# Log-sum-exp of 16,384 rows: another layout of the rows over the partitions, and two stores for one

## Chip, cores and metric

One core of a Trainium2 chip. The metric is device time in microseconds of one execution. Timed runs of one kernel mostly lie within 0.3 us of their median, so that small differences are told by the ratio over several rounds with its 95% interval.

## The reference

```python
# x: (32, 512, 1024) float32, standard normal; result (32, 512)
max_x = np.max(x, axis=-1, keepdims=True)
return (max_x.squeeze(-1) + np.log(np.sum(np.exp(x - max_x), axis=-1))).astype(np.float32)
```

16,384 rows of 4 KiB are read once, 67.1 MB; 64 KB are written.

## The kernel before

The kernel sums plain exponentials, with no maximum taken off, and checks at the end that no sum left the safe range; only if one did would a branch do the exact computation. Each of the 128 partitions owns 128 consecutive rows, 512 KiB of memory; this distance from the first row of one partition to that of the next is called the pitch here. Seventeen groups of rows (16, 16, 16, 15, 14, 10, 9, 8, 6, 4, 4, 3, 2, 2, 1, 1, 1 rows per partition) pass through a ring of 48 rows: SyncE issues the load, ScalarE takes exponentials in place, VectorE or ScalarE's own accumulator forms the sums.

```python
x_rows = x_flat.rearrange("(p c) d -> p c d", p=P)
out_view = out.rearrange("a b -> (a b)").rearrange("(p c) -> p c", p=P)
...
EARLY = 104
...
def load(p0, c0, size):
    step = 4 if c0 in (32, 48) else 1        # third and fourth load in four parts
    return [
        nc.sync.dma_start(
            out=ring[k::step, p0 : p0 + size, :], in_=x_rows[k::step, c0 : c0 + size, :]
        ).ins
        for k in range(step)
    ]
...                                          # in the loop over the loads:
    if c == EARLY + 14:
        nc.scalar.activation(out=res[:, 0:EARLY], in_=sumexp[:, 0:EARLY], func=AF.Ln)
...                                          # after the loop:
nc.scalar.activation(out=res[:, EARLY:NC], in_=sumexp[:, EARLY:NC], func=AF.Ln)
nc.sync.dma_start(out=out_view, in_=res)
```

Two logarithms fill the result: one over columns 0 to 103, taken while the last loads are still coming, one over the last 24 at the very end.

Of the kernel before, what the change touches and what calls it, by code (L numbers as in the profile page):

```python
# [14 lines left out]
def kernel(  # L15
# [5 lines left out]
    nc = tc.nc  # L21
    P = nc.NUM_PARTITIONS
# [6 lines left out]
    x_flat = x.flatten_outer_dims()  # L29
    n, d = x_flat.shape  # L30
    assert n % P == 0
    NC = n // P
    H = d // 2

    x_rows = x_flat.rearrange("(p c) d -> p c d", p=P)
    out_view = out.rearrange("a b -> (a b)").rearrange("(p c) -> p c", p=P)



# [2 lines left out]
    loads = [  # L42
        "R8 R8", "R8 R8", "R8 R8", "R7 R6 A A", "R6 R5 A A A", "R5 R4 A", "R5 R4", "R5 T3",
        "R3 A A A", "R3 A", "R2 T2", "R3", "R1 A", "T2", "T1", "A", "A",
    ]
    loads = [[(op[0], int(op[1:] or 1)) for op in load.split()] for load in loads]
    assert sum(s for ops in loads for _, s in ops) == NC
    ENGINES = [mybir.EngineType.Activation, mybir.EngineType.DVE]
    EARLY = 104
    LATE = 118  # L50
    LAST = NC - 1
# [5 lines left out]
    ring = big.tile([P, RING, d], fp32, name="ring")  # L57
    sumexp = stats.tile([P, NC], fp32, name="sumexp")
    res = stats.tile([P, NC], fp32, name="res")
# [9 lines left out]
    nc.vector.memset(ones, 1.0)  # L69
    nc.vector.memset(far, 100 * HIGH)  # L70

    def load(p0, c0, size):


        step = 4 if c0 in (32, 48) else 1
        return [
            nc.sync.dma_start(
                out=ring[k::step, p0 : p0 + size, :], in_=x_rows[k::step, c0 : c0 + size, :]
            ).ins
            for k in range(step)  # L80
        ]

    def without_wait(ins, group, reason):

        tc.declare_no_dep(ins.ins, group=group, reason=reason)


    def check(c0, c1, i):
        nc.vector.tensor_scalar(  # L89
            out=clamped[:, c0:c1], in0=sumexp[:, c0:c1],  # L90
            scalar1=LOW, scalar2=HIGH, op0=ALU.max, op1=ALU.min,
        )
        nc.vector.scalar_tensor_tensor(  # L93
            out=clamped[:, c0:c1], in0=clamped[:, c0:c1], scalar=0.0, in1=sumexp[:, c0:c1],
            op0=ALU.bypass, op1=ALU.not_equal, accum_out=bad[:, i : i + 1],
        )
        nc.tensor.matmul(count, lhsT=bad[:, i : i + 1], rhs=far, start=i == 0, stop=False)  # L97

    c = 0
    p = 0  # L100
    for ops in loads:
        size = sum(s for _, s in ops)
        if p + size > RING:
            p = 0
        dmas = load(p, c, size)
        if c == 0:
            first_load = dmas[0]
        for how, s in ops:
            v = ring[:, p : p + s, :]
            sums = sumexp[:, c : c + s]  # L110
            if how == "A":
                o = v if c < LAST else last_exp
                exp = nc.scalar.activation(out=o, in_=v, func=AF.Exp, accum_out=sums)  # L113
            else:
                exp = nc.scalar.activation(out=v, in_=v, func=AF.Exp)  # L115
            without_wait(exp, "loads", "the slot's earlier users came before this load")
            without_wait(exp, "exps", "the slot's earlier users came before this load")
            without_wait(exp, "sums", "the slot's earlier users came before this load")
            tc.add_to_no_dep_group("exps", exp.ins)
            added = []  # L120
            if how == "R":
                added = [nc.vector.reduce_sum(out=sums, in_=v, axis=AX.X)]  # L122
            elif how == "T":
                for r in range(s):
                    lo = ring[:, p + r, 0:H]
                    added.append(
                        nc.vector.scalar_tensor_tensor(  # L127
                            out=lo, in0=lo, scalar=1.0, in1=ring[:, p + r, H:d],
                            op0=ALU.mult, op1=ALU.add, accum_out=sums[:, r : r + 1],
                        )  # L130
                    )
            for add in added:
                for dma in dmas:
                    tc.declare_no_dep(add.ins, dma, reason="ScalarE has waited for it")
                without_wait(add, "loads", "they came before this one")
            for add in added:
                tc.add_to_no_dep_group("sums", add.ins)
            c += s
            p += s
            last_row = v  # L140
        for dma in dmas:
            tc.add_to_no_dep_group("loads", dma)
        if c == EARLY + 14:
            nc.scalar.activation(out=res[:, 0:EARLY], in_=sumexp[:, 0:EARLY], func=AF.Ln)  # L144
        if c == LATE + 3:
            check(0, LATE, 0)

    def start_early(program):
# [13 lines left out]
    nc.at_finalize(start_early)  # L162

    nc.scalar.activation(out=res[:, EARLY:NC], in_=sumexp[:, EARLY:NC], func=AF.Ln)  # L164
    nc.sync.dma_start(out=out_view, in_=res)



# [3 lines left out]
        out=bad[:, 2:3], in0=bad[:, 3:4], scalar1=LOG_LOW, scalar2=None, op0=ALU.is_lt  # L172
# [4 lines left out]
    all_fine = nc.values_load(  # L177
        fine[0:1, 0:1], engines=ENGINES, min_val=0, max_val=1,
        skip_runtime_bounds_check_because="a truth value",
    )  # L180
    with tc.If(all_fine < 1, preferred_fallthrough_block=False):
        with tc.tile_critical(sync_engine=mybir.EngineType.Activation):
            with nc.semaphore("landed") as landed, nc.semaphore("ready") as ready:
                rows = 0
                steps = 0
                for c0 in range(0, NC, RING):
                    s = min(RING, NC - c0)
                    v = ring[:, 0:s, :]
                    neg = clamped[:, c0 : c0 + s]
                    if c0:  # L190
                        nc.scalar.wait_ge(ready, steps)
                    nc.scalar.dma_start(out=v, in_=x_rows[:, c0 : c0 + s, :]).then_inc(landed, 16)
                    rows += 16
                    nc.vector.wait_ge(landed, rows)
                    nc.vector.tensor_reduce(
                        out=neg, in_=v, op=ALU.max, axis=AX.X, negate=True
                    ).then_inc(ready, 1)
                    nc.vector.wait_ge(ready, steps + 1)
                    nc.vector.tensor_add(
                        out=v, in0=v, in1=neg[:, :, None].to_broadcast([P, s, d])  # L200
                    ).then_inc(ready, 1)
                    nc.scalar.wait_ge(ready, steps + 2)
                    nc.scalar.activation(out=v, in_=v, func=AF.Exp).then_inc(ready, 1)
                    nc.vector.wait_ge(ready, steps + 3)
                    nc.vector.reduce_sum(
                        out=sumexp[:, c0 : c0 + s], in_=v, axis=AX.X
                    ).then_inc(ready, 1)
                    steps += 4
                nc.scalar.wait_ge(ready, steps)
                nc.scalar.activation(out=res, in_=sumexp, func=AF.Ln).then_inc(ready, 1)  # L210
                nc.vector.wait_ge(ready, steps + 1)
                nc.vector.tensor_sub(out=res, in0=res, in1=clamped).then_inc(ready, 1)
                nc.scalar.wait_ge(ready, steps + 2)
                nc.scalar.dma_start(out=out_view, in_=res).then_inc(landed, 16)
                nc.scalar.wait_ge(landed, rows + 16)


# [28 lines left out]
```

## Time and profile before

| | before |
|---|---|
| time, median (3 runs at first; 6 with the later ones) | 164.42 us (164.14 us) |
| span of the profiled run | 162.2 us |
| busy: DMA queue / VectorE / ScalarE | 96.8% / 75% / 72% |
| loads, first packet to last | 1.01 to 157.92 us |
| store issued, SyncE goes on after it | 159.80, 161.35 us |

The DMA queue is what is full; the two compute engines follow it.

### The profile page before, as it was taken

What the parts mean: (1) busy time and instruction counts of PE and PEld (TensorE: products, weight loads), DVE (VectorE), ACT (ScalarE), POOL (GpSimd) and SP (SyncE); (2) the same over time, 40 slices, a digit from 0 to 9 for tenths busy, and PEclk for the clock granted to TensorE, in tenths of its full rate; (3) what the DMA queues carried; (4) which work ended last, traced back from release to release, by engine and by line L of the source; (5) the groups of instructions that cost most, each with busy time, mean ns of one, the idle gap of its engine ahead of it and who ended that gap; (6) DMA issues with size and microseconds to landing.
All of it is one profiled execution on the core that took longest, in us unless ns stands there. A gap on an engine that the chain in (4) does not pass through costs nothing.

```text
span 162.2 us, 216 instructions
## 1 busy us (share of the span) xinstructions
PE 0.6 (0%) x8; PEld 0.3 (0%) x8; DVE 122.3 (75%) x47; ACT 116.8 (72%) x53; POOL 0.2 (0%) x4
## 2 busy tenths in 40 slices
PE   0000000000000000000000000000000000000001
PEld 0000000000000000000000000000000000000000
DVE  0000000799959999499999995999998999979993
ACT  3000049990799709994499839999969599999993
POOL 0000000000000000000000000000000000000000
DMA  7997997997997999999999999999999999999980
GB/s 259 517 453 323 517 501 307 485 517 323 453 517 323 453 501 394 394 424 485 453 453 396 410 422 414 414 432 436 436 420 436 426 424 410 436 421 411 413 338 20
DMA packets 2690, 67.19 MB, mean 414 GB/s; under 512 B 384, under 2 KB 512, under 8 KB 896
## 3 DMA queue, kind: packets, MB, share of 16 engines
q1 hardware_dynamic: 2688, 67.18, 96.8%
q14 instruction: 2, 0.02, 0.0%
HBM read 67.11 MB, written 0.07 MB: 414 GB/s over the span
## 4 chain that ended last, share of the span: by engine, by line
DMA 64%; DVE 22%; ACT 12%; issue 0%; PE 0%; DVEq 0%
DMA ring<-in_x_dram 64%; DVE sumexp L122 21%; ACT ring L115 12%; DVE ring L127 1%; PE count L174 0%; DVE clamped L89 0%; DVE bad L171 0%; DVE bad L170 0%; DVE clamped L93 0%; DVE fine L176 0%; PE count L175 0%; DVEq L89 0%
## 5 line engine op out<-in xcount | busy, mean ns | idle before, releaser
L122 DVE TENSOR_REDUCE sumexp<-ring 128x8 f32<-128x8192 f32 (+7 forms) x20 | 116.1, 5854 | 36.2 <-ACT ring L115 36.2
L115 ACT ACTIVATE ring<-ring 128x8192 f32<-128x8192 f32 (+7 forms) x24 | 101.7, 4283 | 42.2 <-DMA ring<-in_x_dram 42.2
L113 ACT ACTIVATE ring<-ring 128x1024 f32<-128x1024 f32 x12 | 12.5, 1040 | 0.0
L127 DVE SCALAR_TENSOR_TENSOR ring<-ring 128x512 f32<-128x512 f32 x8 | 5.1, 686 | 0.0
L113 ACT ACTIVATION_READ_ACCUMULATOR ring<-ring 128x1 f32 x12 | 2.2, 186 | 0.0
L68 ACT ACT_TABLE_LOAD x1 | 1.3, 1283 | 0.8 <-PEq L230 0.8
L113 ACT ACTIVATE last_exp<-ring 128x1024 f32<-128x1024 f32 x1 | 1.0, 1013 | 0.0
L97 PE MATMUL count<-far,bad 128*1 128x1 f32 x4 | 0.4, 164 | 159.1 <-DVE clamped L93 159.1
L69 DVE MEMSET ones<- 128x1 f32 x1 | 0.1, 59 | 0.9 <-PEq L230 0.9
L127 DVE DVE_READ_ACCUMULATOR ring<-ring 128x1 f32 x8 | 0.7, 84 | 0.0
L93 DVE SCALAR_TENSOR_TENSOR clamped<-clamped,sumexp 128x118 f32<-128x118 f32 (+1 forms) x2 | 0.5, 226 | 0.1
L89 DVE TENSOR_SCALAR clamped<-sumexp 128x118 f32<-128x118 f32 (+1 forms) x2 | 0.4, 198 | 0.1
L97 PEld LDWEIGHTS count<-far,bad 128*1 128x1 f32 x4 | 0.2, 81 | 159.2 <-DVE clamped L93 159.2
L176 DVE TENSOR_SCALAR fine<-count 1x1 int32<-1x1 f32 x1 | 0.1, 147 | 0.3 <-PE count L175 0.3
L144 ACT ACTIVATE res<-sumexp 128x104 f32<-128x104 f32 x1 | 0.3, 272 | 0.0
L164 ACT ACTIVATE res<-sumexp 128x24 f32<-128x24 f32 x1 | 0.2, 223 | 0.0
L170 DVE TENSOR_REDUCE bad<-ring 128x1 f32<-128x64 f32 x1 | 0.2, 220 | 0.0
L174 PE MATMUL count<-far,bad 128*1 128x1 f32 x2 | 0.2, 164 | 0.2 <-DVE bad L171 0.2
L175 PE MATMUL count<-ones,sumexp 128*1 128x1 f32 x2 | 0.2, 164 | 0.0
L113 ACT ACTIVATION_READ_ACCUMULATOR last_exp<-ring 128x1 f32 x1 | 0.2, 186 | 0.0
L171 DVE TENSOR_SCALAR bad<-bad 128x1 f32<-128x1 f32 x1 | 0.2, 154 | 0.0
L93 DVE DVE_READ_ACCUMULATOR clamped<-clamped,sumexp 128x1 f32 x2 | 0.2, 82 | 0.0
(7 smaller groups left out, 0.7 us busy)
## 6 DMA issues: line engine op xcount, KB each, us to landing
ring<-in_x_dram SPq DMA_DIRECT2D x4, 1920.0 KB, 24.8
ring<-in_x_dram SPq DMA_DIRECT2D x1, 7168.0 KB, 30.1
ring<-in_x_dram SPq DMA_DIRECT2D x1, 5120.0 KB, 31.3
ring<-in_x_dram SPq DMA_DIRECT2D x1, 4608.0 KB, 33.7
ring<-in_x_dram SPq DMA_DIRECT2D x1, 4096.0 KB, 29.3
ring<-in_x_dram SPq DMA_DIRECT2D x2, 2048.0 KB, 32.7
ring<-in_x_dram SPq DMA_DIRECT2D x1, 3072.0 KB, 36.2
ring<-in_x_dram SPq DMA_DIRECT2D x2, 1024.0 KB, 38.8
```

What stands on the lines that cost most here:

```text
L68: nc.scalar.preload_act_table_set("natural_log_exp_and_others")
L89: nc.vector.tensor_scalar(out=clamped[:, c0:c1], in0=sumexp[:, c0:c1], scalar1=LOW, scalar2=HIGH, op0=ALU.max, op1=ALU.min,)
L93: nc.vector.scalar_tensor_tensor(out=clamped[:, c0:c1], in0=clamped[:, c0:c1], scalar=0.0, in1=sumexp[:, c0:c1], op0=ALU.bypass, op1=ALU.n ...
L97: nc.tensor.matmul(count, lhsT=bad[:, i : i + 1], rhs=far, start=i == 0, stop=False)
L113: exp = nc.scalar.activation(out=o, in_=v, func=AF.Exp, accum_out=sums)
L115: exp = nc.scalar.activation(out=v, in_=v, func=AF.Exp)
L122: added = [nc.vector.reduce_sum(out=sums, in_=v, axis=AX.X)]
L127: nc.vector.scalar_tensor_tensor(out=lo, in0=lo, scalar=1.0, in1=ring[:, p + r, H:d], op0=ALU.mult, op1=ALU.add, accum_out=sums[:, r : r + 1],
L144: nc.scalar.activation(out=res[:, 0:EARLY], in_=sumexp[:, 0:EARLY], func=AF.Ln)
L164: nc.scalar.activation(out=res[:, EARLY:NC], in_=sumexp[:, EARLY:NC], func=AF.Ln)
L170: nc.vector.reduce_max(out=bad[:, 3:4], in_=last_row[:, 0, 0 : d // 16], axis=AX.X)
L171: nc.vector.tensor_scalar(out=bad[:, 2:3], in0=bad[:, 3:4], scalar1=LOG_LOW, scalar2=None, op0=ALU.is_lt)
```

## The change

Each partition now owns 120 consecutive rows, a pitch of 480 KiB, from the first 15,360 rows; the last 1,024 rows are given out 8 per partition and are read as the eighth load, into columns 0 to 7. The result then lies in two regions of the output, hence two stores, of 32 and 480 bytes per partition. The intent is to get the 128 streams off a pitch that is a large power of two. The splits of the third to fifth load change from 4, 4, 1 parts to 4, 2, 2.

```diff
-    x_rows = x_flat.rearrange("(p c) d -> p c d", p=P)
-    out_view = out.rearrange("a b -> (a b)").rearrange("(p c) -> p c", p=P)
+    B = 8
+    W = NC - B
+    x_rows = x_flat[0 : P * W].rearrange("(p c) d -> p c d", p=P)
+    x_rest = x_flat[P * W : n].rearrange("(p c) d -> p c d", p=P)
+    out_flat = out.rearrange("a b -> (a b)")
+    out_rows = out_flat[0 : P * W].rearrange("(p c) -> p c", p=P)
+    out_rest = out_flat[P * W : n].rearrange("(p c) -> p c", p=P)
...
-        step = 4 if c0 in (32, 48) else 1
+        step = {2: 4, 3: 2, 4: 2}.get(i, 1)
...
+        if i == REST:                     # REST = 7
+            c = 0
+        else:
+            c = following                 # starts at B
+            following += size
...
-    nc.sync.dma_start(out=out_view, in_=res)
+    nc.sync.dma_start(out=out_rest, in_=res[:, 0:B])
+    nc.sync.dma_start(out=out_rows, in_=res[:, B:NC])
```

The early logarithm's condition now counts `following`, and with it still comes after the same load.

More of the change, by code (lines that the diff above doesn't have):

```diff
@@ L48 @@
     ENGINES = [mybir.EngineType.Activation, mybir.EngineType.DVE]
+    REST = 7
     EARLY = 104
@@ L70, with source, load @@
     nc.vector.memset(far, 100 * HIGH)
-    def load(p0, c0, size):
-        step = 4 if c0 in (32, 48) else 1
+    def source(c0, size):
+        assert c0 >= B or (c0 == 0 and size == B)
+        return x_rows[:, c0 - B : c0 - B + size, :] if c0 >= B else x_rest
+    def load(p0, c0, size, i):
+        step = {2: 4, 3: 2, 4: 2}.get(i, 1)
         return [
             nc.sync.dma_start(
-                out=ring[k::step, p0 : p0 + size, :], in_=x_rows[k::step, c0 : c0 + size, :]
+                out=ring[k::step, p0 : p0 + size, :], in_=source(c0, size)[k::step]
             ).ins
@@ L97, in check @@
         nc.tensor.matmul(count, lhsT=bad[:, i : i + 1], rhs=far, start=i == 0, stop=False)
-    c = 0
+    following = B
     p = 0
-    for ops in loads:
+    for i, ops in enumerate(loads):
         size = sum(s for _, s in ops)
@@ L104 @@
             p = 0
-        dmas = load(p, c, size)
-        if c == 0:
+        if i == REST:
[3 more added lines that the diff above has]
+            following += size
+        dmas = load(p, c, size, i)
+        if i == 0:
             first_load = dmas[0]
@@ L142 @@
             tc.add_to_no_dep_group("loads", dma)
-        if c == EARLY + 14:
+        if following == EARLY + 14:
             nc.scalar.activation(out=res[:, 0:EARLY], in_=sumexp[:, 0:EARLY], func=AF.Ln)
-        if c == LATE + 3:
+        if following == LATE + 3:
             check(0, LATE, 0)
@@ L191 @@
                         nc.scalar.wait_ge(ready, steps)
-                    nc.scalar.dma_start(out=v, in_=x_rows[:, c0 : c0 + s, :]).then_inc(landed, 16)
-                    rows += 16
+                    for c1, s1 in ((0, B), (B, s - B)) if c0 == 0 else ((c0, s),):
+                        nc.scalar.dma_start(
+                            out=ring[:, c1 - c0 : c1 - c0 + s1, :], in_=source(c1, s1)
+                        ).then_inc(landed, 16)
+                        rows += 16
                     nc.vector.wait_ge(landed, rows)
@@ L213 @@
                 nc.scalar.wait_ge(ready, steps + 2)
-                nc.scalar.dma_start(out=out_view, in_=res).then_inc(landed, 16)
-                nc.scalar.wait_ge(landed, rows + 16)
+                nc.scalar.dma_start(out=out_rest, in_=res[:, 0:B]).then_inc(landed, 16)
+                nc.scalar.dma_start(out=out_rows, in_=res[:, B:NC]).then_inc(landed, 16)
+                nc.scalar.wait_ge(landed, rows + 32)
 _INS = ['x']
```

## The prediction

> **What bounds the kernel now.** I began with the page's strip of 40 slices and the totals of the DMA queue, because the change is about the addresses that the loads read.
>
> ```profile
> DMA  7997997997997999999999999999999999999980
> DMA packets 2690, 67.19 MB, mean 414 GB/s; under 512 B 384, under 2 KB 512, under 8 KB 896
> q1 hardware_dynamic: 2688, 67.18, 96.8%
> HBM read 67.11 MB, written 0.07 MB: 414 GB/s over the span
> ```
>
> The reader is to see 96.8%: the 16 DMA engines have packets in flight for all but 5.2 us of the 162.2 us. (The 7s in the first third alternate with 9s because whole 64 KB packets are booked at one point; the same effect gives impossible shares over 1 in short windows.) So I asked for longer stretches, cut where the packet sizes change:
>
> ```profile
> core 0: us, PE busy (x) PEld busy (x) DVE busy (x) ACT busy (x) POOL busy (x), PEclk, DMA share, GB/s
> 0.00:4.50 4.50, 0.00 (x0) 0.00 (x0) 0.09 (x2) 1.28 (x1) 0.20 (x4) 1.00 0.92 320
> 4.50:46.00 41.50, 0.00 (x0) 0.00 (x0) 16.62 (x2) 18.32 (x3) 0.00 (x0) 1.00 1.01 439
> ...
> 46.00:61.00 15.00, 0.00 (x0) 0.00 (x0) 12.97 (x3) 9.57 (x2) 0.00 (x0) 1.00 1.00 433
> ...
> 95.50:140.00 44.50, 0.00 (x0) 0.00 (x0) 42.02 (x13) 40.67 (x20) 0.00 (x0) 1.00 0.99 428
> 140.00:151.00 11.00, 0.00 (x0) 0.00 (x0) 10.04 (x10) 10.97 (x11) 0.00 (x0) 1.00 0.99 419
> ```
>
> Only two stretches are below some 430 GB/s: the first 4.5 us, and the end, where packets shrink to 16, 8 and 4 KB. The single packet records of the trace say why. A 64 KB packet takes 2.418 us in the steady part, which is 27.1 B/ns on one engine, 433.7 GB/s on 16; the 384 packets of that size are all within 0.05 us of it except the first one on each engine (16 of them, 2.97 to 3.46 us, mean 3.22) and one second packet (2.57). A 16 KB packet takes 0.615 us (26.7 B/ns), a 4 KB one 0.161 (25.4), so each packet has some 10 ns of its own. If every packet took the steady time of its size, an engine would be busy 155.54 us; it is busy 156.50 on average. Loads start at 1.01 and end at 157.92, 156.91 us apart. So all that the load stream loses against its own steady speed is about 1 us, 0.81 of it in the first packet (3.22 less 2.42).
>
> Next, is the queue ever empty, or does a compute engine hold it up? The waits of the issuing queue:
>
> ```profile
> SPq L77 <- DVE sumexp L122: 86.0, 7, 24.3
> SPq L77 <- DMA ring<-in_x_dram: 38.6, 4, 18.4
> SPq L165 <- ACT res L164: 18.7, 1, 18.7
> ```
>
> The issuer waits 86.0 us for the reduction that frees ring rows, and yet the engines don't run dry: the fourth load is issued at 46.68 us while the third is landing until about 60.6, and the fifth at 66.00 while the fourth lands until 78.8. The slack is 13 to 14 us, so an issue that is a microsecond earlier or later changes nothing. The chain of waits agrees: 64% of it is DMA, and its DVE and ACT pieces are only the route by which a ring slot was freed.
>
> The last thing is what follows the loads. In order of time:
>
> ```profile
> 158.38 1.01 ACT L113 ACTIVATE last_exp<-ring 128x1024 f32<-128x1024 f32 x1
> ...
> 159.55 0.22 ACT L164 ACTIVATE res<-sumexp 128x24 f32<-128x24 f32 x1
> ...
> 159.80 0.35 SPq L165 DMA_DIRECT2D out_dram<-res  x1
> ```
>
> and the queue's waits after 159 us:
>
> ```profile
> SPq L241 <- ACTq L181: 0.3, 1, 0.3
> SPq L241 <- DMA out_dram<-res: 0.2, 1, 0.2
> ```
>
> The store is issued at 159.80; its packets (27 ns each) run from 160.64 to 161.00, and SyncE, after the branch of the other engines, still waits 0.2 us for it and goes on at 161.35. From there 0.85 us of closing barrier lead to 162.2. So the store's landing is on the path that sets the end, with a slack of only -0.2 us.
>
> **What the Trainium skill says.** "DMA: Bandwidth & Descriptors", section "Latency and other measured facts", has the reason for the change: at a per-partition row pitch of 512 KiB, copies from HBM to HBM ran at 207 GB/s per direction, against 214 at a pitch padded by 4 KiB (with 103 at 4 MiB). This kernel's pitch is 128 rows x 4 KiB = 512 KiB; the change makes it 120 x 4 KiB = 480 KiB. Taken as it stands that is 3% of the load stream. The trace doesn't agree that it is lost here: at 512 KiB the loads run at 433.7 GB/s. The same page, section "Where 436 GB/s comes from", puts the ceiling of the ports into SBUF at 435.2 GB/s; the trace's steady 433.7 is 99.7% of that, so no memory layout has more than 0.3% to give in the steady part. (In the copies there is no SBUF port in the way and both sides have the pitch.) The page's "Specifications" give about 0.6 us to the first byte on this path, which is most of the 0.81 us by which the first packets are longer, and say that transfers under 512 B need a read-modify-write; the store before is of exactly 512 B per partition, and no run so far shows a smaller one to HBM.
>
> **The change part by part.**
> 1. Pitch 480 instead of 512 KiB for 15 of the 16 load groups, and 8 rows per partition (32 KiB each, contiguous) from the tail of the input as the eighth load. Row sizes, order of sizes and ring slots are the same: the load of 8 rows was the eighth before too. So the packets have the same sizes and the steady part takes the same. Possible gain: only the 0.81 us of the start, where all 16 engines begin together on addresses with equal low bits. By the 0.6 us of the skill, about 0.2 of it could be conflict; by the trace alone, anything from 0 to 0.81. I choose 0.25. It would pass through in full, because every later landing, slot and issue moves with it.
> 2. Splits. The third load stays in four parts; the fourth goes from four parts to two, the fifth from one to two: 22 load issues for 23. A further issue costs SyncE 0.33 to 0.6 us, with 13 us of slack. The semaphore that each issue reuses moves by one, to older loads mostly. Worth 0.
> 3. Compute: the same tiles on the same engines; sums, logs and checks are taken at the same places in the sequence (the eighth load now fills columns 0 to 7, still inside the first 104). Worth 0.
> 4. Two stores for one. The 32-byte one goes first, at 159.80 less the gain; the 480-byte one follows it on the same queue. Issues back to back in this trace start 0.37 to 0.48 us apart (113.399, 113.770, 114.249 us), and the second of such a pair takes 0.10 us longer than one alone (0.434 against 0.328). The second store's landing is therefore later by about 0.40, perhaps 0.50. The 128 packets of 32 B take eight places per engine, at 10 to 27 ns each at most 0.2 us, but they run while the second issue is still being written, so none of it adds. A read-modify-write, if it shows, adds perhaps 0.1. As the old landing was already what SyncE waited for, all of it counts: +0.45.
> 5. The branch with the exact maximum is not taken and its instructions cost nothing here beyond what they cost before.
>
> Sum: -0.25 + 0 + 0 + 0.45 = +0.20 us on 164.42, which is 164.62. I say 164.6.
>
> **Rivals.**
> - *The pitch does cost bandwidth, as in the copies.* 3% of 156.9 us would be -4.7 us, some 160.2 with the store. For it: the skill's measurement at this very pitch, and that somebody thought it worth a change. Against it: packets of one size that vary by 0.05 us in 156 us, at the rate of the SBUF ports. A conflict would show as spread. I give it 3%.
> - *The first packets are slow through conflict altogether.* Then 0.8 us come back and the time is 164.42 - 0.8 + 0.45 = 164.1. The first 16 packets' spread (2.97 to 3.46) speaks for it a little; that a first packet must bear the latency which later ones hide behind their predecessors speaks against.
> - *The stores cost more.* If the small writes make the landing wait, the old 1.2 us from issue to the last completion packet may become 2: 164.42 + 1.0 to 1.3 = 165.4 to 165.7. No packet under 512 B other than completion writes is in the trace, so I can't exclude it.
> - *Two parts instead of four load the SBUF ports unevenly.* Another grouping of partitions per engine could slow packets of the fourth and fifth loads, 29 of 128 rows. Against it: the third and fourth loads in four parts ran at 433 GB/s, as fast as the unsplit ones. If it came, 10% of 35 us would be 3.5 us, but slack doesn't help a busy DMA: 168. I give it 2%.
>
> **Range and chances.** The likely terms are a gain of 0 to 0.8 and a cost of 0.35 to 1.0, so -0.45 to +1.0; the three runs before spread over 0.30 us. That gives 163.9 to 165.3 for 8 times in 10. Two per cent is 3.29 us: faster needs a time under 161.13, which only the first rival gives; slower needs 167.71, which only the last one gives. Hence 0.03, 0.95, 0.02.
>
> **What would show it.** In the changed profile the loads' 64 KB packets still take 2.42 us and the rate from 4.5 to 140 us stays at 428 to 439 GB/s (step 1); if it rises above 436 over a long stretch, the ceiling is not what I take it for. The stretch 0 to 4.5 us, now 320 GB/s, shows the gain at the start: 64 KB packets of 2.97 to 3.46 us become shorter or don't. The fourth and fifth loads keep their packet durations (step 2). The last exponential begins near 158.1 (step 3). Two issues of the store 0.35 to 0.5 us apart, and a wait of SyncE for a store of 0.6 to 0.8 us in place of 0.2 show step 4. The prediction is wrong if the middle of the load stream becomes faster or slower, or if the last store lands over 1 us later after the last logarithm than it did.

## More of the kernel before

All runs told here were at a granted clock of 1.0.

Besides the lines in the prediction, one view is needed later: ScalarE's instructions in order of time. In it a line that begins after idle time put down to the DMA gives the moment when a load had landed and been noticed. The first column is the start, the second the duration, and the bracket holds the idle time before it.

```profile
22.32 13.95 ACT L115 ACTIVATE ring<-ring 128x8192 f32<-128x8192 f32 x2 [20.25 <-DMA ring<-in_x_dram]
41.62 13.95 ACT L115 ACTIVATE ring<-ring 128x8192 f32<-128x8192 f32 x2 [5.36 <-DMA ring<-in_x_dram]
61.07 13.95 ACT L115 ACTIVATE ring<-ring 128x8192 f32<-128x8192 f32 x2 [5.49 <-DMA ring<-in_x_dram]
```

The first three loads (8 MB each) were there at 22.32, 41.62 and 61.07 us.

## The result and the profile after

163.91 us (163.61 to 164.16, 6 runs) against 164.14 (164.01 to 164.47, 6 runs): ratio 0.9981, interval 0.9966 to 0.9996. A ratio here is the mean time of one kernel's fast runs over that of the other's of the same rounds, so not quite the ratio of the medians quoted. By the usual 2% it is "the same", as forecast, but the sign is other than predicted: 0.3 us faster where I had 0.2 us slower.

The totals of the changed kernel, the same lines of the page as in the prediction:

```profile
DMA  8995995996996999799999899899999999999980
DMA packets 2818, 67.19 MB, mean 415 GB/s; under 512 B 640, under 2 KB 640, under 8 KB 1024
q1 hardware_dynamic: 2816, 67.18, 97.0%
```

128 packets more, all of them the second store's; 415 GB/s for 414. The stretches, cut at the same times (the last two columns are the DMA's share and GB/s):

```profile
0.00:4.50 4.50, 0.00 (x0) 0.00 (x0) 0.09 (x2) 1.28 (x1) 0.20 (x4) 1.00 0.97 335
4.50:46.00 41.50, 0.00 (x0) 0.00 (x0) 16.90 (x2) 18.56 (x3) 0.00 (x0) 1.00 1.02 444
46.00:61.00 15.00, 0.00 (x0) 0.00 (x0) 12.93 (x3) 9.51 (x3) 0.00 (x0) 1.00 0.96 415
```

The first stretch went from 320 to 335 GB/s. The other two went up by 5 and down by 18, and neither means anything, although 444 is above the 436 and 415 below the 428 that the prediction named as signs (439 stood there before the change): whole 64 KB packets are booked at one moment, and one round of them on 16 engines is 1.05 MB, which is 70 GB/s in a stretch of 15 us. For tenths of a microsecond this view is too coarse. ScalarE's waits for landings are sharp:

```profile
22.04 13.95 ACT L133 ACTIVATE ring<-ring 128x8192 f32<-128x8192 f32 x2 [19.96 <-DMA ring<-in_x_dram]
41.39 13.95 ACT L133 ACTIVATE ring<-ring 128x8192 f32<-128x8192 f32 x2 [5.40 <-DMA ring<-in_x_dram]
60.83 13.95 ACT L133 ACTIVATE ring<-ring 128x8192 f32<-128x8192 f32 x2 [5.49 <-DMA ring<-in_x_dram]
```

Each landing comes 0.23 to 0.28 us earlier, the first one too. So in this pair of traces all of the gain is made before the first load has landed, and it stays to the end: the loads end at 157.69 for 157.92. The packet records agree: the last of the 16 first packets ends at 4.79 us, before at 5.03, while the median 64 KB packet takes 2.418 us in both. The packets of the fourth and fifth load, whose splits changed, keep their median too, 2.267 and 2.116 us; that was the prediction's sign for step 2.

The other surprise is in SyncE's issues in order of time, from 130 us on:

```profile
135.88 0.33 SPq L90 DMA_DIRECT2D ring<-in_x_dram  x1
141.97 0.35 SPq L183 DMA_DIRECT2D out_dram<-res  x1
159.58 0.34 SPq L184 DMA_DIRECT2D out_dram<-res  x1
```

The small store is not at the end at all. It goes out at 141.97, right after the early logarithm, 17.6 us before the large one. Its packets (9 ns each) pass only at 157.1 to 157.7, with the last loads. Only one store is left at the tail, as before. SyncE's waits of that time say the same:

```profile
SPq L184 <- ACT res L182: 13.9, 1, 13.9
...
SPq L183 <- ACT res L162: 1.2, 1, 1.2
...
SPq L264 <- DMA out_dram<-res: 0.3, 1, 0.3
```

L183, the small store, waits for L162, the early logarithm; L184, the large one, for L182, the last. The closing wait for the store is 0.3 us for 0.2, not the 0.6 to 0.8 that I had expected.

### The profile page after: what moved, and what is told of

It is laid out like the page before. It is cut to its first block, busy times and chain, and to the rows that moved or that the text cites. A ratio compares the mean times of both kernels' runs of the same rounds, so it can differ in the third digit from the quotient of the medians.

```text
span 162.0 us, 216 instructions
## 1 busy us (share of the span) xinstructions
PE 0.6 (0%) x8; PEld 0.3 (0%) x8; DVE 122.4 (76%) x47; ACT 116.8 (72%) x53; POOL 0.2 (0%) x4
## 2 busy tenths in 40 slices
DMA packets 2818, 67.19 MB, mean 415 GB/s; under 512 B 640, under 2 KB 640, under 8 KB 1024
## 4 chain that ended last, share of the span: by engine, by line
DMA 63%; DVE 22%; ACT 12%; issue 0%; SPq 0%; PE 0%; DVEq 0%; ACTq 0%
DMA ring<-in_x_dram 63%; DVE sumexp L140 21%; ACT ring L133 12%; DVE ring L145 1%; SPq L90 0%; PE count L193 0%; DVE clamped L102 0%; DVE bad L190 0%; DVE bad L189 0%; DVE clamped L106 0%; DVE fine L195 0%; PE count L194 0%; DVEq L102 0%; ACTq L133 0%
## 5 line engine op out<-in xcount | busy, mean ns | idle before, releaser
L162 ACT ACTIVATE res<-sumexp 128x104 f32<-128x104 f32 x1 | 0.3, 272 | 0.0
L182 ACT ACTIVATE res<-sumexp 128x24 f32<-128x24 f32 x1 | 0.2, 222 | 0.0
```

## The experiments

Theory: the pitch is worth a few tenths of a microsecond at the start, and the second store costs nothing because the early logarithm releases it. Rivals: the splits or the early store make the gain; the start's 0.25 us is luck of one trace; a second store is hidden even at the tail. All runs had five rounds, on two chips, each compared with the kernel before in rounds on the same chip.

### Controls: the changed kernel and the kernel before, again

No edit.

> The changed kernel once more, as a control for size. Theory: the gain is the earlier end of the first packets (4.79 us against 5.03 before) and the small store is off the tail, so 0.997 to 0.999 of before. Rival (the -0.3 us is only the luck of one profile and three rounds): 0.999 to 1.001, and the first packets of this profile end anywhere from 4.7 to 5.1 us.

Measured: 163.63 us against 164.10, ratio 0.9972 (0.9959 to 0.9985). First packets all ended at 4.56 us, loads at 157.46.

> The kernel before against itself, for the noise: 0.999 to 1.001. If the first packets' last end differs from 5.03 us by over 0.1 us in this profile, the start varies from run to run without any change of layout, and the 0.25 us that I saw there says nothing on the layout.

Measured: 164.22 against 164.14, 0.9999 (0.9986 to 1.0013). First packets ended at 5.07 us, loads at 158.16. ScalarE's waits for the first and the third load in this second trace of the kernel before:

```profile
22.38 13.95 ACT L115 ACTIVATE ring<-ring 128x8192 f32<-128x8192 f32 x2 [20.30 <-DMA ring<-in_x_dram]
...
61.27 13.95 ACT L115 ACTIVATE ring<-ring 128x8192 f32<-128x8192 f32 x2 [5.63 <-DMA ring<-in_x_dram]
```

The start is the same as in the first trace within 0.06 us, but the third load lands 0.20 us later. The packet records show where: 52 of the 368 later 64 KB packets took over 2.44 us (up to 2.57), most of them between 47 and 56 us. The trace from which I predicted had 3 of them. So a property that I had taken for a fact of the kernel was a fact of one execution.

### Both stores, old layout

```diff
-    nc.sync.dma_start(out=out_view, in_=res)
+    nc.sync.dma_start(out=out_view[:, 0:8], in_=res[:, 0:8])
+    nc.sync.dma_start(out=out_view[:, 8:NC], in_=res[:, 8:NC])
```

> Before with the two stores of the change (8 columns first, then 120), old layout and splits. Theory: the first store needs only the first logarithm and goes out near 142 us, so nothing is added to the tail: 0.9995 to 1.0005 of before, SyncE goes on about 1.55 to 1.60 us after the issue of the last store. Rival (the early store itself is the gain): 0.998. My prediction's step 4 would have it at +0.45 us, 1.0027.

Measured: 164.40 against 164.10, 1.0014 (1.0001 to 1.0027). A miss: it is slower than the theory has it. The small store does go out at 142.48 us, and the wait for the large one ends 1.56 us after its issue, as with one store of 512 bytes (1.55). What I had not thought of is the closing part: SyncE then waits for its DMA semaphores in a fixed order, about 0.06 us for each instruction. The build hands eight semaphores out in turn. Before, 23 loads and a store make 24 DMAs, and the store has the semaphore that is waited for last; here the last store is the 25th DMA, gets the semaphore of the first load again, and three more of these waits follow it. From the end of the store's wait to the last barrier wait it is 0.92 us for 0.78. That is 0.14 of the measured 0.23 us, and the interval begins at 0.02, so the rest is not resolved. It is clear that the early store is not the gain.

### The two stores swapped, old and new layout

The same two lines in the other order, in the kernel before and in the changed one.

> Before with the two stores in the other order, so that the store of 8 columns (32 B) can only go out after the one of 120 columns, at the tail. Theory: the cost that I predicted, 0.40 to 0.50 us, appears here: 1.0024 to 1.0031. Rival (a second store at the tail is hidden behind the branch and closing waits): under 1.001. Rival (small writes are slow): over 1.004.

> The changed kernel with its two stores swapped, so that the small one is last. Theory: 0.40 to 0.50 us over the changed kernel, 1.0005 to 1.0015 of before, that is the 164.6 of the prediction. Rival (store order is not the step that failed): the same as the changed kernel within 0.1 us.

Measured: 1.0012 (0.9999 to 1.0026) and 0.9984 (0.9971 to 0.9997). Neither tested what it was for. SyncE's issues in the changed kernel with the lines swapped:

```profile
141.98 0.35 SPq L184 DMA_DIRECT2D out_dram<-res  x1
159.58 0.34 SPq L183 DMA_DIRECT2D out_dram<-res  x1
```

L184, now the small store, still comes first: in both swapped builds the store whose data is ready first is issued first, whatever the source says. In effect the two runs repeat the ones above (164.32 and 163.86 us), and count as such.

### Both stores really at the tail

```diff
-    nc.sync.dma_start(out=out_view, in_=res)
+    nc.sync.dma_start(out=out_view[:, 0:120], in_=res[:, 0:120])
+    nc.sync.dma_start(out=out_view[:, 120:NC], in_=res[:, 120:NC])
```

> Before with one store split at column 120 (480 and 32 bytes per partition), old layout and splits. Both parts hold columns of the last logarithm, so both can only go out at the tail, which the two swapped runs did not reach (there the small store went out at 142 us all the same). Theory: the second store's issue comes 0.35 to 0.48 us after the first and its landing ends the program: last issue to SyncE going on 1.55 to 1.60 us, time +0.40 to +0.50 us, 1.0024 to 1.0031, with another 0.1 us possible from the order of the closing waits. Rival (a second store at the tail is hidden): under 1.0015.

Measured: 164.74 against 164.28, 1.0022 (1.0010 to 1.0035), that is +0.36 us with an interval of 0.16 to 0.57. SyncE's issues at the tail, and its wait for the stores after 157 us:

```profile
160.25 0.35 SPq L165 DMA_DIRECT2D out_dram<-res  x1
160.64 0.43 SPq L166 DMA_DIRECT2D out_dram<-res  x1
```

```profile
SPq L242 <- DMA out_dram<-res: 0.9, 1, 0.9
```

The second issue is 0.39 us after the first, its wait ends 1.52 us after it (1.55 with one store), and the wait grew from 0.2 to 0.9 us (a part of it stands where waits for the other engines stood before). Another 0.14 us is the order of the closing waits, 0.92 for 0.78, as there are 25 DMAs again. That is about 0.5 us in this trace. So the price that I set for a second store at the tail, 0.45 us, fits this kernel, though I had not counted the closing waits; the change just doesn't pay it.

### The splits alone

```diff
-        step = {2: 4, 3: 2, 4: 2}.get(i, 1)
+        step = {2: 4, 3: 4}.get(i, 1)
```

> The changed kernel with the old splits (third and fourth load in four parts, fifth whole). Theory (splits are worth 0): as the changed kernel, 0.997 to 0.999 of before. Rival (the gain comes from the splits): 1.000.

Measured: 0.9991 (0.9977 to 1.0004), 164.02 us. Its loads end at 157.61, as the changed kernel's (157.69 and 157.46), so the loads don't care. But with 23 loads and two stores the last store is the 25th DMA, its semaphore comes three places earlier in the closing waits, and from the end of the store's wait to the last barrier wait it is 0.92 us for 0.76. Those 0.16 us are on the path: from the end of the loads to the end of the span it is 4.49 us, for 4.31 to 4.33 in the three traces of the changed kernel. So the new splits have a use that I did not see when I predicted: with 22 loads the two stores again make 24 DMAs, and the last store keeps the last place.

```diff
-        step = 4 if c0 in (32, 48) else 1
+        step = {32: 4, 48: 2, 63: 2}.get(c0, 1)
```

> Before with the new splits alone (4, 2, 2). Theory: 0.9995 to 1.0005. Rival (the splits are the gain): 0.997 to 0.999.

Measured: 1.0012 (0.9999 to 1.0026), 164.39 us. With 23 DMAs the store comes one place earlier, and its closing part is 0.82 us for 0.78; the 0.2 us as a whole are not told from zero. The splits give no gain by themselves.

### The pitch alone

The next three read with another pitch and change nothing else: one store, old splits. Partitions then overlap, so the sums belong to the wrong rows. The comparison with the reference passed all the same: every row of 1,024 normal values has nearly the same log-sum-exp, so the tolerance doesn't notice. That check is blind to a permutation here.

```diff
-    x_rows = x_flat.rearrange("(p c) d -> p c d", p=P)
+    PITCH = 120                                     # also 127 and 64
+    x_rows = bass.AP(tensor=x_flat.tensor, offset=x_flat.offset,
+                     ap=[[PITCH * d, P], [d, NC], [1, d]])
```

> Before with the pitch of the loads alone set to 120 rows (480 KiB); partitions then overlap by 8 rows, so the result is wrong on purpose; one store, old splits, everything else as before. Theory (pitch alone makes the gain): first packets all ended by 4.6 to 4.8 us, under 10 stray slow 64 KB packets after them, loads end at 157.4 to 157.7, time 0.996 to 0.998 of before. Rival (tail of the input, splits or stores make it): 1.000 and 30 or more stray packets.

Measured: 163.89 against 164.28, 0.9975 (0.9962 to 0.9988). ScalarE's waits for the first three loads:

```profile
21.95 13.95 ACT L116 ACTIVATE ring<-ring 128x8192 f32<-128x8192 f32 x2 [19.88 <-DMA ring<-in_x_dram]
41.29 13.95 ACT L116 ACTIVATE ring<-ring 128x8192 f32<-128x8192 f32 x2 [5.39 <-DMA ring<-in_x_dram]
60.73 13.95 ACT L116 ACTIVATE ring<-ring 128x8192 f32<-128x8192 f32 x2 [5.48 <-DMA ring<-in_x_dram]
```

The landings are those of the changed kernel, a tenth of a microsecond earlier still. The pitch alone makes the gain.

> The same with a pitch of 127 rows (508 KiB, wrong on purpose): 4 KiB off the power of two. Theory (equal low address bits collide): as with 120 rows, 0.996 to 0.998, few stray packets. Rival (the pitch must be well off 512 KiB): between it and before, 0.998 to 1.000.

Measured: 0.9976 (0.9963 to 0.9990), 163.79 us. 4 KiB off 512 KiB is as good as 32 KiB off.

> The same with a pitch of 64 rows (256 KiB, wrong on purpose), again a power of two. Theory (a power of two collides): as before, first packets ended at 4.9 to 5.1 us and 30 or more stray slow packets, 0.999 to 1.001. Rival (only the size 512 KiB, or the total range of memory, matters): 0.996 to 0.998.

Measured: 0.9969 (0.9957 to 0.9982), 163.78 us, with not one later packet over 2.44 us. ScalarE's waits for the first and the third load:

```profile
21.99 13.95 ACT L116 ACTIVATE ring<-ring 128x8192 f32<-128x8192 f32 x2 [19.92 <-DMA ring<-in_x_dram]
...
60.73 13.95 ACT L116 ACTIVATE ring<-ring 128x8192 f32<-128x8192 f32 x2 [5.48 <-DMA ring<-in_x_dram]
```

Here my theory fell: 256 KiB is a power of two as well and shows no such cost. Among the pitches tried it is 512 KiB that costs. One thing is not separated: at 64 rows the loads also span only half of the input and read most rows twice, so the smaller range of memory stays a rival to the pitch in this run.

### Blocks without any pitch

```diff
-                out=ring[k::step, p0 : p0 + size, :], in_=x_rows[k::step, c0 : c0 + size, :]
+                out=ring[k::step, p0 : p0 + size, :], in_=x_flat[P * c0 : P * (c0 + size)].rearrange(
+                    "(p c) d -> p c d", p=P
+                )[k::step]
```

The result is permuted and so wrong.

> Before, but each load reads one contiguous block of rows (pitch equal to the row group: 64 KiB for the big loads), so no 512 KiB pitch is left anywhere; the output is permuted and so wrong on purpose. Theory (SBUF ports limit the steady part, layout acts at the start at most): steady 64 KB packets stay at 2.418 us, time 0.997 to 1.000 of before. Rival (the pitch costs bandwidth): under 0.98, and packets shorter than 2.41 us.

Measured: 163.68 against 164.14, 0.9978 (0.9964 to 0.9991); the median 64 KB packet takes 2.418 us as ever. Not better than 480 KiB; none of the layouts tried gives more.

### The traces side by side

From the packet records of all 14 traces. "Later slow" counts, of the 368 later 64 KB packets, those of over 2.44 us.

| pitch | traces | last of the first 16 packets ends, us | later slow | loads end, us |
|---|---|---|---|---|
| 512 KiB | before, before_again, s_early, s_late, b_split, s_tail | 4.89 to 5.12, mean 5.04 | 3, 52, 54, 85, 35, 24 | 157.92 to 158.36, mean 158.15 |
| 480 KiB | after, after_again, a_late, a_split, p120 | 4.56 to 4.79, mean 4.70 | 3, 0, 1, 1, 2 | 157.46 to 157.69, mean 157.60 |
| 508 KiB, 256 KiB, blocks | p127, p64, blocks | 4.75, 4.71, 4.62 | 4, 0, 0 | 157.66, 157.61, 157.57 |

In the first and the last of these columns no trace at 512 KiB reaches into the two other groups, and both sides hold traces from both chips. The loads end 0.55 us earlier at 480 than at 512 KiB: 0.34 by the start, and the other 0.21 later. That the bursts of slow packets make the later part shows in the time from the end of the first packets to the end of the loads: it is 152.88 to 152.95 us in all nine traces with at most 4 slow packets, the first one at 512 KiB among them, and 152.97 to 153.35 us in the five with 24 or more.

## Why the prediction was wrong

**Step 4 failed, the two stores.** It said that the 32-byte store "goes first, at 159.80 less the gain" and that the 480-byte one follows 0.40 to 0.50 us behind, +0.45. The size fits two stores at the tail: 0.39 us between issues and 0.14 in the closing waits when I put them there. But columns 0 to 7 are finished by the early logarithm, so the small store left at 141.97 us, and what stayed was one store of 480 bytes, whose wait ended 0.04 us later than that of one of 512. In step 3 I had noted that the rest's columns lie "inside the first 104" and did not follow it to the store. That one term gives the sum its wrong sign.

**Step 1 had the right cause, the pitch, and the right place, the start, but too small a size and a mechanism that the runs don't bear out.** Predicted -0.25, all at the start. Measured -0.55 in the end of the loads: 0.34 at the start and 0.21 from bursts of packets that take 2.44 to 2.86 instead of 2.42 us. My last line named "the middle of the load stream becomes faster" as a sign of being wrong, and over all traces it came, by these 0.21 us. The 0.25 was picked out of 0 to 0.81; the estimate behind it put a latency to the first byte inside the first packet, which no run shows (that packet starts 1.01 us after the first issue). That the first pair of traces had about 0.25 at the start is luck. Inside the start it was not the first packets' length that shrank (their mean is 3.24 us at 480 KiB and 3.07 at 512); the last of the 16 finishes earlier, and the load has landed only with the slowest engine: the sixteen completions of the first load came at 21.45 to 22.29 us before, and ScalarE began at 22.32. Equal low address bits don't explain it alone, since 256 KiB has them as well. (A slip without weight: 16 of the 17 load groups get the pitch of 480 KiB, not 15 of 16.)

**The first rival was dismissed on one trace.** "A conflict would show as spread" was a fair test, and the trace in hand showed none. Five of the six traces at 512 KiB show it, and I had the sixth. The rival's size, 3%, was far off all the same: 0.55 of 156.9 us is 0.35%, since the steady 27.1 B/ns per engine holds in every layout.

**Step 2, splits: right for the loads, not quite for the end.** They move no landing that these runs resolve, but with the stores they decide which semaphore the last store gets, and so how many closing waits follow its landing: up to 0.16 us. In the change itself that number stays as it was, so this does not shift the sum.

**Step 3 held.** The last exponential began at 158.16 us, predicted near 158.1.

With the measured terms the sum is -0.55 + 0.04 and about -0.02 for the closing part (0.76 us for 0.78), about -0.5 us. The three timed sets of the changed kernel (0.9981, 0.9972, and 0.9984 with the stores swapped in the source) average 0.9979, some -0.35 us, and the pitch alone at 120 rows gives 0.9975, -0.41. The traces are one execution each and the loads' end scatters by 0.1 to 0.2 us, so sum and times agree within their noise. No experiment beats the changed kernel clearly. What stays open is why 512 KiB costs and 256 KiB doesn't: no run here looks inside the memory.

## What to carry to other kernels

Before adding up the costs of two stores, look for what finishes the data of each: here the early one cost the tail nothing but a place in the closing waits. For that place, count the DMAs: here 25 in place of 24 cost 0.14 to 0.16 us. When a conclusion rests on the spread within one trace ("no packet is slow"), take a second trace first, for rare bursts may miss one execution. In a kernel whose DMA engines are full, look at the slowest of the 16 engines at the first landing, not at mean GB/s, which cannot show tenths of a microsecond.

## What the Trainium skill lacked or had wrong

- "DMA: Bandwidth & Descriptors", section "Latency and other measured facts": the entry on the row pitch is for copies between memory and memory, 3% at 512 KiB. For loads into SBUF at 512 KiB these runs show 0.35% (loads end at 158.15 us for 157.60), with 508, 480 and 256 KiB free of it; the page says nothing of 256 KiB. That 4 KiB off the power of two is enough agrees (0.9976).
- The same page, "Specifications", has a read-modify-write for transfers under 512 B, without a cost. Here the wait for a last store of 480 bytes per partition ended 1.58 to 1.60 us after the issue where the pieces lie end to end (four traces of the new layout), 1.56 where they lie 512 bytes apart (two traces), and 1.55 to 1.56 with 512 bytes (seven); with 32 bytes behind a larger store it was 1.52. So at most 0.04 us, and size alone doesn't explain that.
- No page that I read says that the order in which SyncE passes its DMA semaphores at the end counts: from the end of the store's wait to the last barrier wait it took 0.76 to 0.79 us where the last store's came last, 0.82 where one more followed, and 0.92 where three did.
